# Recurrent heads: the decay levels within 32 tokens computed in 32-column strips of TensorE, in a compact tile

## The chip, the cores and the metric

One core of a Trainium2 chip. The metric is the time of one execution on the device, in microseconds (us); the median of several runs is compared.

## The reference, cut to what matters

The kernel is a decoder trunk on 256 tokens with a model width of 2048: one layer of two parallel head groups, one recurrent layer, and norms around them. The change touches one of the head groups, a gated linear recurrence (16 heads, 128 keys and 128 values each):

```python
def hgrn2(q, fz, v, lb, gain):
    f = lb + (1.0 - lb) * sigmoid(fz)      # decay per key and token
    k = (1.0 - lb) * sigmoid(-fz)
    b = cumsum(log(max(f, TINY)))          # along the tokens of a chunk
    # within a chunk, for s <= t:
    att[t, s] = sum_k silu(q)[t, k] * k[s, k] * exp(b[t, k] - b[s, k])
    o[t] = sum_s att[t, s] * v[s] + what earlier chunks left
```

The decay between two tokens differs for each key, so `att` is no plain product of q and k.

## The kernel before

All weights arrive in chunks of 512 KB, are split by ScalarE (cast, L136) and VectorE (remainder, L137) into two fp32r halves, and are multiplied on TensorE (L183, L185, L209) in units of 256 columns. The order of TensorE's instructions is the order in which the program writes them; the other engines are scheduled by a planner. Side work runs as generators: each `yield n` hands control back, and after n more chunks of the running unit (`tick`, one chunk being about 16 products) the generator goes on. So the small products of a head stand in TensorE's queue between chunks of big ones.

The 16 heads go in 8 pairs, one generator `hgrn` per pair (L670 to L828), with 128 keys on the partitions and four tiles `j` of 128 tokens (two heads, two halves of the 256 tokens). `att` (keys' tokens s on the partitions, four tiles of 128 query tokens t) is built by levels, so that no logarithm is needed. On each level the queries and keys, `qg` and `kg`, carry the decay up to the edge of blocks of w tokens; a product of both gives the entries between neighbouring blocks, and the entries of that level are picked out of the product by a mask. In order: single tokens (L697: diagonal and odd tokens), w=2 and w=8 (L746, three distances at once, in the 192 columns of `qx`), w=32 (L780), w=64 (L791), the far tile (L798). Each of L697 and L746 multiplies all 128 tokens s by 192 columns for each j, in two banks of two tiles, though only entries within blocks of 32 tokens are kept. VectorE picks: L700 and L702 for the single tokens, L769 (six predicated copies a level, whole rows of `att` under masks of 192 columns), L784 for w=32. The level w=64 is copied by ScalarE (L793). Between the products VectorE multiplies `qg` and `kg` by the decays of the level (L738 to L760, `grow` L710 and L711).

fp32 products are recorded as two weight loads and two matmuls each.

Of the kernel before, what the change touches and what calls it, by code (L numbers as in the profile page):

```python
# [9 lines left out]
F32 = mybir.dt.float32  # L10
F32R = mybir.dt.float32r
U8 = mybir.dt.uint8
AF = mybir.ActivationFunctionType
ALU = mybir.AluOpType
# [3 lines left out]
P = 128  # L18
# [17 lines left out]
V_PEK, V_PEV = 240, 272  # L36
NV = 304

C_ID, C_D0, C_D1, C_ROW, C_HEAD, NCONST = 0, 128, 400, 928, 929, 931


def shape_constants():

    c = np.zeros((P, NCONST), np.float32)
    i = np.arange(P)
    c[:, C_ID:C_ID + P] = np.eye(P)

    def follows(w, d):

        n = 4 if d else 2  # L50
        t = i[(i // w) % n >= max(d, 1)]
        return ((i[:, None] // (n * w) == t[None, :] // (n * w)) & (i[:, None] // w == t[None, :] // w - max(d, 1)))

    m = np.zeros((P, 4, 192), np.float32)
    m[:, 0, :64] = follows(1, 0)
    for r, w in ((1, 2), (2, 8)):
        m[:, r] = np.concatenate([follows(w, d) for d in (1, 2, 3)], axis=1)
    m[:, 3, :64] = follows(32, 0)
    ends = np.arange(16) * 16 + 31

    def dist(t, s):
        d = (t[:, None] - s[None, :]).astype(np.float32)
        return np.where(d >= 0, -d, np.float32(NEG))

    cmp0, cmp1 = dist(i, ends), dist(i + P, ends)
    cmp0[:, 15] = cmp1[:, 15] = NEG
    cmp0[:31] = 0.0
    near, far = dist(i, i), dist(i + P, i)
    c[:, C_D0:C_D0 + 272] = np.concatenate([cmp0, near, near], 1)
    c[:, C_D1:C_D1 + 528] = np.concatenate([cmp1, far, far, near, near], 1)  # L70
    c[:, C_ROW] = i >= 31
    for h in range(2):
        c[:, C_HEAD + h] = i // 16 % 2 == h
    return c, m
# [3 lines left out]
def trunk_kernel(ctx: ExitStack, tc: tile.TileContext, x, vecs, consts, blocks, w_in, w_vg, w_out,  # L78
                 w1, w2, o_in, o_gate, o_out, out):
    nc = tc.nc  # L80
    V, S, TE = nc.vector, nc.scalar, nc.tensor

    ctx.enter_context(tc.manual_schedule(engines={mybir.EngineType.PE}))
    cst = ctx.enter_context(tc.tile_pool(name="cst", bufs=1))
# [5 lines left out]
    def bank():  # L90
        return sd.tile([P, 512], F32, name="sb")
# [4 lines left out]
    con = cst.tile([P, NCONST], F32, name="con")  # L96
# [8 lines left out]
    ident = con[:, C_ID:C_ID + P]  # L105
# [263 lines left out]
    cm = tc.alloc_tile_pool(name="cm", bufs=2)  # L369
# [7 lines left out]
            normed(kc[:, 32 * u:32 * u + 32].rearrange("p (g m) b -> p g (m b)", g=2), ps, cm)  # L377
        kcs.append(kc)
    nc.sync.dma_start(con, consts)
    masks = cst.tile([P, 4, 192], U8, name="masks")  # L380
    cst.tile([P, 8], F32, name="pad")

    lb = cst.tile([P, KT], F32, name="lb")
    lb1 = cst.tile([P, KT], F32, name="lb1")
    mk = cm.tile([P, 4, 192], F32, name="mk", bufs=1)
    nc.sync.dma_start(mk, blocks)
    V.tensor_copy(masks, mk)
    e = cm.tile([P, KT], F32, name="e", bufs=1)
# [74 lines left out]
    for br, u0 in ((0, 44), (1, 48)):  # L463
        for u in range(2):
            ps = even_unit(u0 + u)
# [174 lines left out]
    def hgrn_pair(p, ps_f, ps_q):  # L640
# [9 lines left out]
        for h in range(2):  # L650
# [6 lines left out]
        normed(g, ps, hg)  # L657
        s = hg.tile([P, 2, T], F32, name="sg")
        S.activation(s, g, AF.Sigmoid)
        q = hg.tile([P, 4, 192], F32, name="q")  # L660
        V.tensor_tensor(q[:, :, 0:P], g.rearrange("p h (j t) -> p (h j) t", t=P),
                        s.rearrange("p h (j t) -> p (h j) t", t=P), op=ALU.mult)

        v = hg.tile([P, 2, 2 * UC], F32, name="v") if p % 2 == 0 else values[0]
        values[:] = [v]
# [4 lines left out]
    def hgrn(p, q, f, k, v):  # L670
# [1 line left out]
            return t.rearrange("p j (n a w) -> p (j n) a w", a=2, w=w)  # L672


        qe = q[:, :, 0:P].rearrange("p j (n a) -> p j n a", a=2)
        fe = f.rearrange("p j (n a) -> p j n a", a=2)
        qo = q[:, :, P:192]
        qg = hg.tile([P, 4, P], F32, name="qg")
        kg = hg.tile([P, 4, P], F32, name="kg")
        qge = qg.rearrange("p j (n a) -> p j n a", a=2)  # L680
        kge = kg.rearrange("p j (n a) -> p j n a", a=2)
        ke = k.rearrange("p j (n a) -> p j n a", a=2)
        V.tensor_tensor(qo, qe[:, :, :, 1], fe[:, :, :, 1], op=ALU.mult)
        V.tensor_tensor(qge[:, :, :, 0], qe[:, :, :, 0], fe[:, :, :, 0], op=ALU.mult)
        V.tensor_tensor(qge[:, :, :, 1], qo, fe[:, :, :, 0], op=ALU.mult)
        V.tensor_tensor(kge[:, :, :, 0], ke[:, :, :, 0], fe[:, :, :, 1], op=ALU.mult)
        V.tensor_copy(kge[:, :, :, 1], ke[:, :, :, 1])
        gend = hg.tile([P, 4 * 64], F32, name="g2")
        V.tensor_tensor(gend.rearrange("p (j n) -> p j n", j=4), fe[:, :, :, 0], fe[:, :, :, 1], op=ALU.mult)
        att = hg.tile([P, 4, P], F32, name="att")  # L690
        yield 3
        odd = att.rearrange("p j (n a) -> p j n a", a=2)[:, :, :, 1]
        for b in range(2):
            ps = bank()
            for i in range(2):
                j = 2 * b + i
                TE.matmul(ps[:, 192 * i:192 * i + 192], k[:, j], q[:, j], start=(i == 0), stop=(i == 1),  # L697
                          skip_group_check=True)
            pv = ps[:, :384].rearrange("p (j c) -> p j c", j=2)
            V.tensor_tensor(att[:, 2 * b:2 * b + 2], pv[:, :, 0:P],  # L700
                            ident.unsqueeze(1).broadcast_to([P, 2, P]), op=ALU.mult)
            V.copy_predicated(odd[:, 2 * b:2 * b + 2], masks[:, 0, 0:64].unsqueeze(1).broadcast_to([P, 2, 64]),  # L702
                              pv[:, :, P:192])

        def grow(w, gend):

# [9 lines left out]

        for m, w in ((1, 2), (2, 8)):

            n = P // (4 * w)
            qx = hg.tile([P, 4, 192], F32, name="qx")  # L720
            x1_ = qx[:, :, 0:96].rearrange("p j (n c) -> p j n c", n=n)
            x2_ = qx[:, :, 96:160].rearrange("p j (n c) -> p j n c", n=n)
            x3_ = qx[:, :, 160:192].rearrange("p j (n c) -> p j n c", n=n)
            qv = qg.rearrange("p j (n c) -> p j n c", n=n)
            kv_ = kg.rearrange("p j (n c) -> p j n c", n=n)
            gv = gend.rearrange("p (j n a) -> p j n a", j=4, a=4)

            def q_(b):
                return qv[:, :, :, b * w:b * w + w]
# [2 lines left out]
                return kv_[:, :, :, b * w:b * w + w]  # L732

            def g_(b):
                return gv[:, :, :, b:b + 1].broadcast_to([P, 4, n, w])

            S.copy(x1_, qv[:, :, :, w:])
            V.tensor_tensor(x2_[:, :, :, 0:w], q_(2), g_(1), op=ALU.mult)  # L738
            V.tensor_tensor(x2_[:, :, :, w:], q_(3), g_(2), op=ALU.mult)
            V.tensor_tensor(x3_, x2_[:, :, :, w:], g_(1), op=ALU.mult)  # L740
            yield 1
            pss = []
            for h in range(2):
                ps = bank()
                for i in range(2):
                    TE.matmul(ps[:P - w, 192 * i:192 * i + 192], kg[:, 2 * h + i, 0:P - w], qx[:, 2 * h + i],  # L746
                              start=(i == 0), stop=(i == 1), skip_group_check=True)
                pss.append(ps)
            V.tensor_tensor(q_(1), q_(1), g_(0), op=ALU.mult)
            V.tensor_tensor(q_(2), x2_[:, :, :, 0:w], g_(0), op=ALU.mult)  # L750
            V.tensor_tensor(q_(3), x3_, g_(0), op=ALU.mult)
            g2 = hg.tile([P, 3, 4 * n], F32, name=f"g{w}")
            gf = gend.rearrange("p (n a) -> p n a", a=4)
            V.tensor_tensor(g2[:, 0], gf[:, :, 2], gf[:, :, 3], op=ALU.mult)
            V.tensor_tensor(g2[:, 1], gf[:, :, 1], g2[:, 0], op=ALU.mult)
            V.tensor_tensor(g2[:, 2], gf[:, :, 0], g2[:, 1], op=ALU.mult)
            V.tensor_tensor(k_(2), k_(2), g_(3), op=ALU.mult)
            for b in range(2):
                gb = g2[:, 1 - b].rearrange("p (j n) -> p j n", j=4).unsqueeze(3).broadcast_to([P, 4, n, w])
                V.tensor_tensor(k_(b), k_(b), gb, op=ALU.mult)  # L760
            gend = g2[:, 2]
            s1 = P - w
            for h in range(2):
                av = att[:s1, 2 * h:2 * h + 2].rearrange("p j (n c) -> p j n c", n=n)
                pv = pss[h][:s1, 0:384].rearrange("p (j c) -> p j c", j=2)
                c0 = 0
                for d in range(1, 4):
                    cols = 32 * (4 - d)
                    V.copy_predicated(av[:, :, :, d * w:],  # L769
                                      masks[:s1, m, c0:c0 + cols].rearrange("p (n c) -> p n c", n=n).unsqueeze(1)  # L770
                                      .broadcast_to([s1, 2, n, cols // n]),
                                      pv[:, :, c0:c0 + cols].rearrange("p j (n c) -> p j n c", n=n))
                    c0 += cols
            if w == 2:
                yield 1
        yield 1
        ps = bank()
        w = 32
        for j in range(4):
            TE.matmul(ps[:P - w, 64 * j:64 * j + 64], kg[:, j, 0:P - w],  # L780
                      qg[:, j].rearrange("p (n a w) -> p n a w", a=2, w=w)[:, :, 1],
                      start=(j == 0), stop=(j == 3), skip_group_check=True)
        gend = grow(w, gend)
        V.copy_predicated(att[:P - w].rearrange("p j (n a w) -> p j n a w", a=2, w=w)[:, :, :, 1],  # L784
                          masks[:P - w, 3, 0:64].rearrange("p (n w) -> p n w", w=w).unsqueeze(1)
                          .broadcast_to([P - w, 4, 2, w]),
                          ps[:P - w, 0:256].rearrange("p (j n w) -> p j n w", j=4, w=w))
        yield 1
        ps = bank()
        for j in range(4):  # L790
            TE.matmul(ps[:64, 64 * j:64 * j + 64], kg[:, j, 0:64], qg[:, j, 64:128],  # L791
                      start=(j == 0), stop=(j == 3), skip_group_check=True)
        S.copy(att[:64, :, 64:128], ps[:64, :256].rearrange("p (j c) -> p j c", j=4))  # L793
        grow(64, gend)
        yield 1
        ps = bank()
# [232 lines left out]
```

## Time and profile before

| what | value |
|---|---|
| median of 3 runs | 1375.11 us (1373.91 to 1375.12) |
| profiled execution, whole | 1374.71 us |
| its span, first to last instruction | 1372.93 us |
| mean granted TensorE clock over the span | 0.995 |
| stretch of the recurrent heads | 420 to 850 us |

The profiled execution is a run of its own; its span leaves out what lies before the first and behind the last instruction. PE is TensorE's matmuls, PEld its weight loads, DVE VectorE, ACT ScalarE, SP the engine that issues the transfers.

### The profile page before, as it was taken

To read this page: it belongs to the slowest core of one execution; us is meant where nothing else is said; L and a number is where in the kernel's file an instruction comes from. 1 tells how busy PE (TensorE), PEld (TensorE's weight loads), DVE (VectorE), ACT (ScalarE), POOL (GpSimd) and SP (SyncE) were. 2 spreads that over 40 slices of the span, in tenths; PEclk is the share of its full clock that TensorE was granted. 3 is DMA by queue.
4 is the path that set the end of the run, shared out by engine and by line. 5 is a ranking of instruction groups with operands and counts; after the bars stand their busy time and mean duration, and the time that the engine had idled before them with its cause. 6 is when DMAs were issued, how large, how long until landed. Compare 5 with 4: busy or idle time off the path is not lost.

```text
span 1372.9 us, 20842 instructions
## 1 busy us (share of the span) xinstructions
PE 1350.2 (98%) x7970; PEld 1189.9 (87%) x7970; DVE 1030.2 (75%) x1755; ACT 801.4 (58%) x1187; POOL 0.2 (0%) x4
## 2 busy tenths in 40 slices
PE   7999999999999999999999999999999999999996
PEld 6899888988998888888888888888888888888884
DVE  7645478888878765577969687776688988886655
ACT  6435466667664543445444455554559899986442
POOL 0000000000000000000000000000000000000000
PEclk9999999999999999999999999999999999999998
DMA  7765654444445556655445454566665665565662
GB/s 270 249 203 156 195 172 152 154 139 153 140 139 171 187 174 211 191 167 172 140 154 158 149 166 157 187 189 193 197 202 169 188 199 166 184 198 171 185 188 87
DMA packets 77251, 240.93 MB, mean 175 GB/s; under 512 B 7520, under 2 KB 13920, under 8 KB 77152
## 3 DMA queue, kind: packets, MB, share of 16 engines
q1 hardware_dynamic: 77152, 239.61, 55.4%
q8 instruction: 62, 1.02, 0.3%
q14 instruction: 37, 0.30, 0.1%
HBM read 237.48 MB, written 2.10 MB: 174 GB/s over the span
## 4 chain that ended last, share of the span: by engine, by line
PE 96%; DVE 2%; DMA 0%; ACT 0%; issue 0%; SPq 0%; DVEq 0%; ACTq 0%
PE ps L183 50%; PE ps L185 25%; PE ps L209 9%; PE sb L151 2%; PE sb L149 2%; PE sb L150 2%; PE sb L746 2%; PE sb L429 1%; PE sb L552 1%; PE sb L697 1%; DMA wr<-in_w_in 0%; DVE w L137 0%; PE sb L780 0%; DVE part L322 0%; PE sb L791 0%
## 5 line engine op out<-in xcount | busy, mean ns | idle before, releaser
L183 PE MATMUL ps<-hx,w 128*128 128x512 f32 x2176 | 756.5, 400 | 8.6 <-DVE hx L237 7.7
L136 ACT CAST w<-wr 128x1024 fp32r<-128x1024 f32 (+2 forms) x437 | 454.9, 1043 | 499.3 <-PE ps L185 287.1
L137 DVE TENSOR_TENSOR w<-wr,w 128x1024 fp32r<-128x1024 f32 (+2 forms) x437 | 530.7, 1217 | 263.8 <-ACT w L136 262.3
L185 PE MATMUL ps<-hx,w 128*128 128x256 f32 x2176 | 568.6, 280 | 0.5 <-DVE w L137 0.4
L183 PEld LDWEIGHTS ps<-hx,w 128*128 128x128 f32 x2176 | 391.6, 188 | 83.0 <-DVE hx L237 8.2
L185 PEld LDWEIGHTS ps<-hx,w 128*128 128x128 f32 x2176 | 411.4, 189 | 24.1 <-DVE w L137 1.4
L183 PE MATMUL ps<-yx,w 128*128 128x512 f32 x832 | 263.0, 395 | 0.0
L185 PE MATMUL ps<-yx,w 128*128 128x256 f32 x832 | 180.8, 280 | 0.0
L185 PEld LDWEIGHTS ps<-yx,w 128*128 128x128 f32 x832 | 147.0, 188 | 16.0
L183 PEld LDWEIGHTS ps<-yx,w 128*128 128x128 f32 x832 | 142.5, 188 | 20.1
L209 PE MATMUL ps<-w,hx 128*128 128x512 f32 (+1 forms) x576 | 128.0, 377 | 0.0
L209 PEld LDWEIGHTS ps<-w,hx 128*128 128x128 f32 x576 | 100.3, 189 | 17.4
L226 ACT COPY sg<-ps 128x512 f32<-128x512 f32 x68 | 39.3, 578 | 2.0 <-DVE ssum L324 1.2
L528 ACT ACTIVATE pr<-pr,mx 128x16 f32<-128x16 f32 (+2 forms) x96 | 37.8, 396 | 3.3 <-DVE mx L525 3.3
L228 DVE TENSOR_TENSOR tmp<-tmp,rB 128x512 f32<-128x512 f32 x46 | 31.8, 690 | 1.2
L227 DVE TENSOR_TENSOR tmp<-ps,sg 128x512 f32<-128x512 f32 x46 | 31.4, 683 | 0.8 <-ACT sg L226 0.7
L769 DVE COPY_PREDICATED att<-masks,sb 126x192 f32<-126x192 uint8 (+3 forms) x96 | 25.6, 319 | 8.2 <-PE sb L746 7.8
L875 DVE SCALAR_TENSOR_TENSOR xc<-xp,vec,xc 128x256 f32<-128x256 f32 x60 | 25.5, 479 | 0.1
L746 PE MATMUL sb<-qx,kg 128*120 128x192 f32 (+1 forms) x128 | 23.4, 326 | 0.0
L151 PE MATMUL sb<-xch,w 128*128 128x256 f32 x80 | 22.6, 282 | 0.0
L517 DVE SCALAR_TENSOR_TENSOR pr<-con,sb 128x272 f32<-128x272 f32 (+1 forms) x48 | 18.9, 428 | 4.9 <-PE sb L151 4.9
L149 PE MATMUL sb<-xch,w 128*128 128x256 f32 x80 | 22.6, 282 | 0.0
(236 smaller groups left out, 1214.7 us busy)
## 6 DMA issues: line engine op xcount, KB each, us to landing
wr<-in_w_in SPq DMA_DIRECT2D x235, 512.0 KB, 3.8
wr<-in_o_in SPq DMA_DIRECT2D x80, 512.0 KB, 4.2
wr<-in_w_out SPq DMA_DIRECT2D x64, 512.0 KB, 3.7
wr<-in_o_out SPq DMA_DIRECT2D x40, 512.0 KB, 3.6
wr<-in_o_gate SPq DMA_DIRECT2D x10, 512.0 KB, 3.6
w<-in_w SPq DMA_DIRECT2D x8, 512.0 KB, 4.8
wr<-in_w_vg SPq DMA_DIRECT2D x5, 456.0 KB, 3.3
tmp<-in_x SPq DMA_DIRECT2D x8, 256.0 KB, 3.5
```

Source lines behind the costliest of these rows:

```text
L136: S.copy(dst_h, src)
L137: V.tensor_tensor(dst_l, src, dst_h, op=ALU.subtract)
L149: TE.matmul(o, ah, bh, start=start, stop=False, skip_group_check=True)
L151: TE.matmul(o, al, bh, start=False, stop=stop, skip_group_check=True)
L183: TE.matmul(ps[:, n], wk, a, start=(c == 0 and k == 0), stop=stop, skip_group_check=True)
L185: TE.matmul(ps[:, n, 0], wk, a[:, 0], start=False, stop=stop, skip_group_check=True)
L209: TE.matmul(o, a[:, sa, ts], w[:, sw, :, k], start=(c == 0 and k == 0 and i == 0), stop=(c * kc + k == KT - 1 and i == 2), skip_group_chec ...
L226: S.copy(t, ps[:, :, 1])
L227: V.tensor_tensor(dst, ps[:, :, 0], t, op=ALU.add)
L228: V.tensor_tensor(dst, dst, rB2(), op=ALU.mult)
L528: S.activation(branch(h, br), branch(h, br), AF.Exp, bias=mx[:, h, br:br + 1], scale=SCALE, accum_out=zs[:, h, br:br + 1])
L746: TE.matmul(ps[:P - w, 192 * i:192 * i + 192], kg[:, 2 * h + i, 0:P - w], qx[:, 2 * h + i], start=(i == 0), stop=(i == 1), skip_group_chec ...
```

## The change

The entries within blocks of 32 tokens are now computed by blocks alone. q (16 blocks of 32 tokens over the four tiles) and `qx` are laid out as 16 blocks of 48 columns: for each block its 32 tokens and 16 odd ones, or the 48 columns of the three distances. A new function `in_blocks` makes, for each tile j and each block m, a product of the 32 keys' tokens of the block (32 weight columns) with those 48 columns, and puts it on the partitions 32m to 32m+31 of one bank: 16 products of 32 by 48 take the place of four of 128 by 192. The result is compact, 4 tiles of 32 columns, in the new tile `near`; the masks shrink to 48 columns, and each predicated copy serves all four tiles at once. Behind w=8 one VectorE product with a mask of blocks spreads `near` over the whole rows of `att`.

The level w=32 becomes eight products of 32 by 32, on the partitions 0 to 31 and 64 to 95, and two ScalarE copies in the place of the predicated copy L784. The level w=64 keeps its four products, two on the partitions 0 to 63 and two on 64 to 127 in turn, with two ScalarE copies in the place of one. The waits of the generators stay.

```diff
@@ shape_constants
     def follows(w, d):
 
-        n = 4 if d else 2
-        t = i[(i // w) % n >= max(d, 1)]
-        return ((i[:, None] // (n * w) == t[None, :] // (n * w)) & (i[:, None] // w == t[None, :] // w - max(d, 1)))
-
-    m = np.zeros((P, 4, 192), np.float32)
...
+        n, u = 4 if d else 2, i[:32]
+        t = u[(u // w) % n >= max(d, 1)]
+        s = (i % 32)[:, None]
+        return (s // (n * w) == t[None, :] // (n * w)) & (s // w == t[None, :] // w - max(d, 1))
+
+    m = np.zeros((P, 3, 48), np.float32)
...
+    c[:, C_I32:C_I32 + 32] = i[:, None] % 32 == i[None, :32]
+    c[:, C_BLK:C_BLK + 4] = i[:, None] // 32 == i[None, :4]
...
@@ hgrn_pair
-        q = hg.tile([P, 4, 192], F32, name="q")
-        V.tensor_tensor(q[:, :, 0:P], g.rearrange("p h (j t) -> p (h j) t", t=P),
-                        s.rearrange("p h (j t) -> p (h j) t", t=P), op=ALU.mult)
+
+        q = hg.tile([P, 16, 48], F32, name="q")
+        V.tensor_tensor(q[:, :, 0:32], g.rearrange("p h (b t) -> p (h b) t", t=32),
+                        s.rearrange("p h (b t) -> p (h b) t", t=32), op=ALU.mult)
...
@@ hgrn
         att = hg.tile([P, 4, P], F32, name="att")
+        near = hg.tile([P, 4, 32], F32, name="near")
+
+        def in_blocks(kk, qq):
+
+            ps = bank()
+            for j in range(4):
+                for m in range(4):
+                    bs = slice(32 * m, 32 * m + 32)
+                    TE.matmul(ps[bs, 48 * j:48 * j + 48], kk[:, j, bs], qq[:, 4 * j + m], start=(j == 0), stop=(j == 3),
+                              skip_group_check=True)
+            return ps[:, 0:192].rearrange("p (j c) -> p j c", j=4)
+
         yield 3
-        odd = att.rearrange("p j (n a) -> p j n a", a=2)[:, :, :, 1]
-        for b in range(2):
...
+        pv = in_blocks(k, q)
+        V.tensor_tensor(near, pv[:, :, 0:32], con[:, C_I32:C_I32 + 32].unsqueeze(1).broadcast_to([P, 4, 32]),
+                        op=ALU.mult)
+        V.copy_predicated(near.rearrange("p j (n a) -> p j n a", a=2)[:, :, :, 1],
+                          masks[:, 0, 0:16].unsqueeze(1).broadcast_to([P, 4, 16]), pv[:, :, 32:48])
...
-            n = P // (4 * w)
-            qx = hg.tile([P, 4, 192], F32, name="qx")
...
+            n = 32 // (4 * w)
+            qx = hg.tile([P, 16, 48], F32, name="qx")
...
             yield 1
-            pss = []
-            for h in range(2):
-                ps = bank()
...
+            pv = in_blocks(kg, qx)
             V.tensor_tensor(q_(1), q_(1), g_(0), op=ALU.mult)
...
-            for h in range(2):
-                av = att[:s1, 2 * h:2 * h + 2].rearrange("p j (n c) -> p j n c", n=n)
...
+            nv = near.rearrange("p j (n c) -> p j n c", n=n)
+            c0 = 0
+            for d in range(1, 4):
+                cols = 8 * (4 - d)
+                V.copy_predicated(nv[:, :, :, d * w:],
+                                  masks[:, m, c0:c0 + cols].rearrange("p (n c) -> p n c", n=n).unsqueeze(1)
+                                  .broadcast_to([P, 4, n, cols // n]),
+                                  pv[:, :, c0:c0 + cols].rearrange("p j (n c) -> p j n c", n=n))
+                c0 += cols
             if w == 2:
                 yield 1
+
+        V.tensor_tensor(att.rearrange("p j (m t) -> p j m t", m=4), near.unsqueeze(2).broadcast_to([P, 4, 4, 32]),
+                        con[:, C_BLK:C_BLK + 4].unsqueeze(1).unsqueeze(3).broadcast_to([P, 4, 4, 32]), op=ALU.mult)
         yield 1
         ps = bank()
         w = 32
         for j in range(4):
-            TE.matmul(ps[:P - w, 64 * j:64 * j + 64], kg[:, j, 0:P - w],
-                      qg[:, j].rearrange("p (n a w) -> p n a w", a=2, w=w)[:, :, 1],
-                      start=(j == 0), stop=(j == 3), skip_group_check=True)
+            for s0 in (0, 64):
+                TE.matmul(ps[s0:s0 + w, w * j:w * j + w], kg[:, j, s0:s0 + w], qg[:, j, s0 + w:s0 + 2 * w],
+                          start=(j == 0), stop=(j == 3), skip_group_check=True)
+        for s0 in (0, 64):
+            S.copy(att[s0:s0 + w, :, s0 + w:s0 + 2 * w], ps[s0:s0 + w, 0:P].rearrange("p (j t) -> p j t", j=4))
         gend = grow(w, gend)
-        V.copy_predicated(att[:P - w].rearrange("p j (n a w) -> p j n a w", a=2, w=w)[:, :, :, 1],
...
         yield 1
         ps = bank()
-        for j in range(4):
-            TE.matmul(ps[:64, 64 * j:64 * j + 64], kg[:, j, 0:64], qg[:, j, 64:128],
-                      start=(j == 0), stop=(j == 3), skip_group_check=True)
-        S.copy(att[:64, :, 64:128], ps[:64, :256].rearrange("p (j c) -> p j c", j=4))
+        for h in range(2):
+            for j in range(2):
+                TE.matmul(ps[64 * j:64 * j + 64, 64 * h:64 * h + 64], kg[:, 2 * h + j, 0:64], qg[:, 2 * h + j, 64:128],
+                          start=(h == 0), stop=(h == 1), skip_group_check=True)
+        ah = att.rearrange("p (h j) t -> p h j t", j=2)
+        for j in range(2):
+            S.copy(ah[:64, :, j, 64:128], ps[64 * j:64 * j + 64, 0:P].rearrange("p (h c) -> p h c", h=2))
         grow(64, gend)
```

## Rows read from the trace of the kernel before

**Rows 1.** The page, busy time by engine, share of the span, instructions.
```profile
PE 1350.2 (98%) x7970; PEld 1189.9 (87%) x7970; DVE 1030.2 (75%) x1755; ACT 801.4 (58%) x1187; POOL 0.2 (0%) x4
```

**Rows 2.** Waits of TensorE: total us, times, longest.
```profile
PE ps L183 <- DVE hx L237: 7.7, 2, 7.1
PE sb L924 <- ACT sg L948: 1.6, 2, 1.4
```

**Rows 3.** Busy us by engine, 420 to 850 us; behind them clock and DMA.
```profile
420.00:850.00 430.00, 430.00 (x2484) 376.66 (x2483) 324.34 (x665) 205.49 (x259) 0.00 (x0) 1.00 0.54 168
```

**Rows 4.** Chain of waits, first pair of heads: start us, us, what.
```profile
423.86 1.30 PE sb L697 x8
...
427.90 1.30 PE sb L746 x8
...
435.96 2.73 PE ps L209 x12
438.69 0.65 PE sb L780 x8
439.34 2.82 PE ps L209 x12
442.16 0.61 PE sb L791 x8
442.77 0.43 PE ps L183
443.20 0.12 PE ps L185
443.32 0.23 PE ps L183
```

**Rows 5.** TensorE's groups by shape, 400 to 850 us: busy us, mean ns | idle.
```profile
L697 PE MATMUL sb<-q,k 128*128 128x192 f32 x64 | 11.7, 325 | 0.0
L746 PE MATMUL sb<-qx,kg 128*126 128x192 f32 x64 | 11.7, 325 | 0.0
...
L780 PE MATMUL sb<-qg,kg 128*96 128x64 f32 x64 | 6.5, 244 | 0.0
```

**Rows 6.** L791: its durations (ns least/median/most); timeline, from 442.09 and from 442.32.
```profile
L791 PE MATMUL sb<-qg,kg x64: 222/222/270, 442.1 to 829.8; 128*64 128x64 f32 x64
...
442.09 0.68 PE L791 MATMUL sb<-qg,kg 128*64 128x64 f32 x8
442.09 0.54 PEld L791 LDWEIGHTS sb<-qg,kg 128*64 128x64 f32 x8 [0.35 <-issue]
442.32 0.46 PE L791 MATMUL sb<-qg,kg 128*64 128x64 f32 x5
```

**Rows 7.** Chain of waits, products with 128 weight and 66 moving columns.
```profile
58.23 1.83 PE sb L429 x16
```

**Rows 8.** Timeline, 35.2 to 35.75 us: the first products after a wait.
```profile
35.35 0.19 PEld L183 LDWEIGHTS ps<-hx,w 128*128 128x128 f32 x1 [1.02 <-PE sb L311]
35.38 0.47 PE L183 MATMUL ps<-hx,w 128*128 128x512 f32 x1 [0.96 <-DVE kc L227]
```

**Rows 9.** Line 746: weight loads, and the waits its sequencer took up (PEldq).
```profile
L746 PEld LDWEIGHTS sb<-qx,kg x128: 180/186/188, 427.5 to 822.6; 128*126 128x126 f32 x64, 128*120 128x120 f32 x64
...
L746 PEldq EVENT_SEMAPHORE  x20: 51/51/51, 424.6 to 818.5; - x20
```

**Rows 10.** Timeline around L780, first and last pair.
```profile
437.11 0.49 DVE L760 TENSOR_TENSOR kg<-kg,g 128x128 f32<-128x128 f32 x2
...
438.31 0.90 PEld L780 LDWEIGHTS sb<-qg,kg 128*96 128x96 f32 x8
...
824.87 0.49 DVE L760 TENSOR_TENSOR kg<-kg,g 128x128 f32<-128x128 f32 x2
...
825.60 0.79 PEld L780 LDWEIGHTS sb<-qg,kg 128*96 128x96 f32 x8
```

**Rows 11.** VectorE's groups, 420 to 850 us by shape; the first from the page.
```profile
L769 DVE COPY_PREDICATED att<-masks,sb 126x192 f32<-126x192 uint8 (+3 forms) x96 | 25.6, 319 | 8.2 <-PE sb L746 7.8
...
L702 DVE COPY_PREDICATED att<-masks,sb 128x128 f32<-128x128 uint8 x16 | 7.1, 442 | 0.0
L700 DVE TENSOR_TENSOR att<-sb,con 128x256 f32<-128x256 f32 x16 | 7.0, 437 | 0.0
...
L661 DVE TENSOR_TENSOR q<-tmp,sg 128x512 f32<-128x512 f32 x8 | 5.5, 685 | 0.0
...
L769 DVE COPY_PREDICATED att<-masks,sb 126x128 f32<-126x128 uint8 x16 | 4.7, 292 | 0.0
...
L769 DVE COPY_PREDICATED att<-masks,sb 120x64 f32<-120x64 uint8 x16 | 3.6, 226 | 0.2
L784 DVE COPY_PREDICATED att<-masks,sb 96x256 f32<-96x256 uint8 x8 | 3.5, 437 | 0.0
```

More of the change, by code (lines that the diff above doesn't have):

```diff
@@ L37 @@
 NV = 304
-C_ID, C_D0, C_D1, C_ROW, C_HEAD, NCONST = 0, 128, 400, 928, 929, 931
+C_ID, C_D0, C_D1, C_ROW, C_HEAD, C_I32, C_BLK, NCONST = 0, 128, 400, 928, 929, 931, 963, 967
 def shape_constants():
@@ L48, in follows @@
     def follows(w, d):
-        n = 4 if d else 2
-        t = i[(i // w) % n >= max(d, 1)]
-        return ((i[:, None] // (n * w) == t[None, :] // (n * w)) & (i[:, None] // w == t[None, :] // w - max(d, 1)))
-    m = np.zeros((P, 4, 192), np.float32)
-    m[:, 0, :64] = follows(1, 0)
+        n, u = 4 if d else 2, i[:32]
[3 more added lines that the diff above has]
+    m = np.zeros((P, 3, 48), np.float32)
+    m[:, 0, :16] = follows(1, 0)
     for r, w in ((1, 2), (2, 8)):
         m[:, r] = np.concatenate([follows(w, d) for d in (1, 2, 3)], axis=1)
-    m[:, 3, :64] = follows(32, 0)
+    c[:, C_I32:C_I32 + 32] = i[:, None] % 32 == i[None, :32]
+    c[:, C_BLK:C_BLK + 4] = i[:, None] // 32 == i[None, :4]
     ends = np.arange(16) * 16 + 31
@@ L379, in trunk_kernel @@
     nc.sync.dma_start(con, consts)
-    masks = cst.tile([P, 4, 192], U8, name="masks")
-    cst.tile([P, 8], F32, name="pad")
+    masks = cst.tile([P, 3, 48], U8, name="masks")
+    cst.tile([P, 32], F32, name="pad")
     lb = cst.tile([P, KT], F32, name="lb")
     lb1 = cst.tile([P, KT], F32, name="lb1")
-    mk = cm.tile([P, 4, 192], F32, name="mk", bufs=1)
+    mk = cm.tile([P, 3, 48], F32, name="mk", bufs=1)
     nc.sync.dma_start(mk, blocks)
@@ L672, in halves @@
             return t.rearrange("p j (n a w) -> p (j n) a w", a=2, w=w)
-        qe = q[:, :, 0:P].rearrange("p j (n a) -> p j n a", a=2)
-        fe = f.rearrange("p j (n a) -> p j n a", a=2)
-        qo = q[:, :, P:192]
+        qe = q[:, :, 0:32].rearrange("p m (n a) -> p m n a", a=2)
+        fe = f.rearrange("p j (m n a) -> p (j m) n a", n=16, a=2)
+        qo = q[:, :, 32:48]
         qg = hg.tile([P, 4, P], F32, name="qg")
         kg = hg.tile([P, 4, P], F32, name="kg")
-        qge = qg.rearrange("p j (n a) -> p j n a", a=2)
+        qge = qg.rearrange("p j (m n a) -> p (j m) n a", n=16, a=2)
         kge = kg.rearrange("p j (n a) -> p j n a", a=2)
         ke = k.rearrange("p j (n a) -> p j n a", a=2)
+        fk = f.rearrange("p j (n a) -> p j n a", a=2)
         V.tensor_tensor(qo, qe[:, :, :, 1], fe[:, :, :, 1], op=ALU.mult)
@@ L685, in hgrn @@
         V.tensor_tensor(qge[:, :, :, 1], qo, fe[:, :, :, 0], op=ALU.mult)
-        V.tensor_tensor(kge[:, :, :, 0], ke[:, :, :, 0], fe[:, :, :, 1], op=ALU.mult)
+        V.tensor_tensor(kge[:, :, :, 0], ke[:, :, :, 0], fk[:, :, :, 1], op=ALU.mult)
         V.tensor_copy(kge[:, :, :, 1], ke[:, :, :, 1])
         gend = hg.tile([P, 4 * 64], F32, name="g2")
-        V.tensor_tensor(gend.rearrange("p (j n) -> p j n", j=4), fe[:, :, :, 0], fe[:, :, :, 1], op=ALU.mult)
+        V.tensor_tensor(gend.rearrange("p (j n) -> p j n", j=4), fk[:, :, :, 0], fk[:, :, :, 1], op=ALU.mult)
         att = hg.tile([P, 4, P], F32, name="att")
-        yield 3
-        odd = att.rearrange("p j (n a) -> p j n a", a=2)[:, :, :, 1]
-        for b in range(2):
-            ps = bank()
[L695 to L703, printed above, removed]
+        near = hg.tile([P, 4, 32], F32, name="near")
[7 more added lines that the diff above has]
+            return ps[:, 0:192].rearrange("p (j c) -> p j c", j=4)
+        yield 3
+        pv = in_blocks(k, q)
[3 more added lines that the diff above has]
+                          masks[:, 0, 0:16].unsqueeze(1).broadcast_to([P, 4, 16]), pv[:, :, 32:48])
         def grow(w, gend):
@@ L717, in hgrn @@
         for m, w in ((1, 2), (2, 8)):
-            n = P // (4 * w)
-            qx = hg.tile([P, 4, 192], F32, name="qx")
[L721 to L726, printed above, removed]
+            n = 32 // (4 * w)
+            qx = hg.tile([P, 16, 48], F32, name="qx")
+            x1_ = qx[:, :, 0:24].rearrange("p m (n c) -> p m n c", n=n)
+            x2_ = qx[:, :, 24:40].rearrange("p m (n c) -> p m n c", n=n)
+            x3_ = qx[:, :, 40:48].rearrange("p m (n c) -> p m n c", n=n)
+            qv = qg.rearrange("p j (m n c) -> p (j m) n c", m=4, n=n)
+            kv_ = kg.rearrange("p j (m n c) -> p (j m) n c", m=4, n=n)
+            gv = gend.rearrange("p (m n a) -> p m n a", m=16, a=4)
             def q_(b):
@@ L734, in g_ @@
             def g_(b):
-                return gv[:, :, :, b:b + 1].broadcast_to([P, 4, n, w])
+                return gv[:, :, :, b:b + 1].broadcast_to([P, 16, n, w])
             S.copy(x1_, qv[:, :, :, w:])
@@ L741, in hgrn @@
             yield 1
-            pss = []
-            for h in range(2):
[L744 to L748, printed above, removed]
+            pv = in_blocks(kg, qx)
             V.tensor_tensor(q_(1), q_(1), g_(0), op=ALU.mult)
@@ L751, in hgrn @@
             V.tensor_tensor(q_(3), x3_, g_(0), op=ALU.mult)
-            g2 = hg.tile([P, 3, 4 * n], F32, name=f"g{w}")
+            g2 = hg.tile([P, 3, 16 * n], F32, name=f"g{w}")
             gf = gend.rearrange("p (n a) -> p n a", a=4)
@@ L758, in hgrn @@
             for b in range(2):
-                gb = g2[:, 1 - b].rearrange("p (j n) -> p j n", j=4).unsqueeze(3).broadcast_to([P, 4, n, w])
+                gb = g2[:, 1 - b].rearrange("p (m n) -> p m n", m=16).unsqueeze(3).broadcast_to([P, 16, n, w])
                 V.tensor_tensor(k_(b), k_(b), gb, op=ALU.mult)
             gend = g2[:, 2]
-            s1 = P - w
-            for h in range(2):
-                av = att[:s1, 2 * h:2 * h + 2].rearrange("p j (n c) -> p j n c", n=n)
[L765 to L773, printed above, removed]
+            nv = near.rearrange("p j (n c) -> p j n c", n=n)
[7 more added lines that the diff above has]
+                c0 += cols
             if w == 2:
                 yield 1
+        V.tensor_tensor(att.rearrange("p j (m t) -> p j m t", m=4), near.unsqueeze(2).broadcast_to([P, 4, 4, 32]),
+                        con[:, C_BLK:C_BLK + 4].unsqueeze(1).unsqueeze(3).broadcast_to([P, 4, 4, 32]), op=ALU.mult)
         yield 1
```

3 lines of the change are left out of this document (removed).

## Prediction

> **What bounds the kernel now.** I read the page first: TensorE's matmuls are busy for 98% of the span, its weight loads for 87%, VectorE for 75% [rows 1]. A busy matmul engine can still be waiting, so the waits come next: the longest of TensorE's, 7.7 us, falls on a line of the first norm, long before the change, and the next, 1.6, on the last norm, long after it [rows 2]. [...] Last the chain of waits through one pair of heads, which gives the price of every block of products that the change touches, in place [rows 4].
>
> **What the old products cost.** Each fp32 product is two weight loads and two matmuls in the records, so a level's four products per pair of heads stand as x8; 64 records over eight pairs are one block each [rows 5]. The token-diagonal level and the levels w=2 and w=8 take 1.30 us each [rows 4]: 162 ns a record for 192 moving columns, 0.85 ns a column, so there the moving side sets the pace. The w=32 level takes 0.65 us, and the products behind it 0.08 more than the same twelve take elsewhere (2.82 against 2.74): 0.73 us [rows 4]. With the other pairs, some of which lose less behind it, I take 0.71. The w=64 level takes 0.61, and the product behind it 0.43 in place of 0.23: 0.81 us [rows 4].
>
> The w=64 block shows more. It is the one whose output has 64 partitions. Its steady pace is (0.46 - 0.222)/4, about 58 ns a record [rows 6], so 8 records explain 0.47 of 0.81; the weight loads stood idle for 0.35 us before it, with nothing awaited [rows 6], while the other blocks' loads run under the matmul before. I read 0.34 us per block as the price of going over to half an array and back. [...]
>
> **What the new products cost.** Per pair of heads each of the three levels becomes 16 products of 32 weight columns and 48 moving columns, 32 records; w=32 becomes 8 products of 32 by 32, 16 records; w=64 keeps 8 records but puts neighbours in different halves of the array. So three blocks and the w=32 block now pay for a change of mode too. In 32 columns its first exposed weight load is shorter by about 25 ns, so I take 0.31 us for each.
>
> Pace of one record, from rows. Weights: 128 columns take 1.83/16 = 114 ns [rows 7] and 64 take 58 [rows 6], so 32 take about 30. Moving: 48 x 0.85 = 41, with a few ns of gap 45. What no row shows is whether a product in one strip runs beside one in another, for every product before sits in the same columns as its neighbour. This is the open cost:
>
> - No overlap: 45 ns a record, the slower of the two sides. The level costs 32 x 45 + 310 = 1.75 us against 1.30.
> - Full overlap: the two records of one product share a strip and follow each other (45 ns in all), then the next strip may start. 16 x 45 + 310 = 1.03 us.
> - Overlap, but fed by the sequencer. After an empty queue a matmul started 30 ns behind its weight load [rows 8], whereas with a filled queue both start together [rows 6]; so one instruction takes the sequencer about 30 ns. A wait of the first w=2 block was taken up at 424.6 for loads at 427.5 [rows 9], twelve pairs ahead at 229 ns; the last at 818.5, for a block that begins at about 821.5, seventeen pairs at 172 ns. So the queue holds about 33 instructions. A level now has 64: 33 are there, 31 x 31 ns = 0.96 us must pass for the rest. 0.96 + 0.31 = 1.27 us, 0.03 less than before.
> - A floor: the shortest pace on record is 58 ns [rows 6]. If that is a price per record and not that of 64 columns, a level costs 32 x 58 + 310 = 2.17 us.
>
> I take the third. Weight loads and matmuls already run beside each other in one half array (58 ns, not their sum), so the array does take separate work at once, and the 30 ns row is the only one of an unfilled queue. The choice between overlap and none has no row at all, which is why both ends stay in the range.
>
> With the third: three levels -0.03 each, -0.09. Level w=32: the sequencer is held by VectorE's last factor until about 0.7 us before the block [rows 10], so some 22 of 32 instructions are ready when its products start; 10 x 31 + 310 = 0.62 against 0.71, -0.09. Level w=64: its 16 instructions are all in the queue, and two halves overlap: 0.23 in place of 0.47, -0.23. Sum -0.41 us per pair, -3.3 us for eight.
>
> **The other engines.** VectorE loses the diagonal product (437 ns twice), the first predicated copy (about as long, twice), 12 copies (25.6 us over all pairs) and the w=32 copy (437 ns) [rows 11], some 43 us. It gains a product and seven shorter copies of 32 to 128 elements, at 0.22 to 0.3 us as rows of 64 to 128 elements show [rows 11], and a spread over 512 elements of SBUF at about 0.69 [rows 11], 2.7 us a pair. That is 21 us less on an engine with 106 idle us in the stretch [rows 3]: I cost it at nothing, since TensorE waits for it nowhere there. ScalarE gains three short copies a pair beside 225 idle us [rows 3], also nothing. Two of them wait for the spread and for the w=32 block, and weight casts stand behind them in ScalarE's queue; a cast that is late by less than a tick is hidden by the weight buffers ahead of TensorE, which wait on nothing in the stretch; without that cover it would cost its wait, a few tenths of a us a pair. One margin is thin: VectorE's last factor before w=32 ends at 437.60 and is wanted at 438.31, in the last pair at 825.36 and 825.60 [rows 10]. These factors keep their counts of elements, and follow the end of the w=8 block as before, so the margin stays; if their new layout cost 20 ns more each, nine of them would take 0.18 of the 0.24 us. The other new thing queued behind them, the spread, is wanted only by the last products of the head, several ticks later. The smaller masks and the slightly longer constants are loaded before 40 us, where nothing waits for them: nothing either way.
>
> **The rivals.**
> 1. *Strips take turns.* 1.75 against 1.30 three times, +1.35; w=32 16 x 30 + 310 = 0.79 against 0.71, +0.08; w=64 unchanged. +1.43 us a pair, +11.4 us: 1386.5. For it: the moving side is one stream wherever a row shows it, 0.85 ns a column. Against: nothing that a row shows. It decides from 31 ns a record up (that is where 32 records and the change of mode reach 1.30).
> 2. *Full overlap, the queue keeps up.* 1.03, -0.27 three times; w=32 8 x 32 + 310 = 0.57, -0.14; w=64 -0.23. -1.18 a pair, -9.4: 1365.7. For it: load and matmul start together when the queue is full [rows 6]. Against: the 30 ns of rows 8. [...]
> 3. *A floor for every small product.* 2.17 against 1.30, +0.87 three times; w=32 16 x 58 + 310 = 1.24, +0.53; +3.13 a pair, +25.0: 1400.1. For it: 58 is the shortest pace on record; against: 64 columns alone explain it. [...]
> 4. *Matmuls overlap, weight loads go in single file.* 30 ns a record: levels 1.27, w=32 0.79, w=64 unchanged: -0.1 us, 1375.0. The change then does nothing for the time.
>
> **How the numbers follow.** The sum is made against the profiled execution: 1374.71 us, of which 1372.93 are the span and 1.8 lie around it. -3.3 gives 1371.4; the median of the runs is 0.40 above that execution, so 1371.8. Chances: the forecast 0.32, full overlap 0.22, loads in file 0.08, turns 0.25, a floor 0.13. A measurement of this kernel tells a change from none at about 0.2%, 2.75 us. The forecast lies just beyond that, so I split it 0.19 faster to 0.13 same. Faster: 0.22 + 0.19 = 0.41. Same: 0.13 and 0.06 of loads in file: 0.19. Slower: 0.25 + 0.13 + 0.02 = 0.40. The range leaves out the floor and little else: from 1.5 under full overlap to some 2 over turns, 1364 to 1389. The forecast's own range is 1369 to 1374.
>
> **What would show it.** In the chain, a level's block as x32 at about 0.96 us plus a first product behind it of 0.43 in place of 0.23; starts 30 ns apart in its second half if the sequencer feeds it, evenly 45 if strips take turns, 58 if there is a floor; pairs of starts 41 ns and a few ns apart if strips overlap in full. Idle time of the weight loads before each of the five narrow blocks of a pair (0.3 us) shows the change of mode, and its absence would make me wrong by up to 0.3 x 32 = 10 us to the good. VectorE busy about 20 us less, with TensorE still without idle time between 420 and 850 us; a wait for a factor at w=32 would show the thin margin gone. [...]

## Result and profile after

The changed kernel takes 1358.32 us (median of 4 runs, 1358.12 to 1359.10) against 1375.11 in the same comparison: a ratio of 0.9879, 95% interval 0.9868 to 0.9891, or 16.8 us less. The forecast was 1371.8, its range 1364 to 1389. The sign was right, the size lies below the range.

The page of the changed kernel, busy time by engine [rows 1]:
```profile
span 1356.3 us, 22071 instructions
## 1 busy us (share of the span) xinstructions
PE 1333.5 (98%) x8610; PEld 1165.7 (86%) x8610; DVE 1011.4 (75%) x1691; ACT 807.2 (60%) x1211; POOL 0.2 (0%) x4
```
TensorE has 640 records more, 80 for each pair of heads, and is busy for 16.7 us less; the span is 16.6 us shorter. Its waits and the stretch of the heads, the first view as in [rows 2], the second as in [rows 3]:
```profile
PE ps L185 <- DVE hx L239: 7.8, 2, 7.5
PE sb L928 <- ACT sg L952: 1.6, 2, 1.4
...
415.00:850.00 435.00, 435.00 (x3237) 368.56 (x3236) 322.77 (x626) 223.03 (x297) 0.00 (x0) 1.00 0.55 176
```
The waits are the old ones. TensorE never stands still while the heads run (busy for 435.00 us of 435.00), at the same granted clock of 1.00. So the time went where TensorE's own blocks became shorter. The chain of waits through the first pair, to be laid beside [rows 4]:
```profile
424.57 0.48 PE sb L703 x32
425.04 2.99 PE ps L211 x12
428.04 0.48 PE sb L703 x32
428.51 5.77 PE ps L211 x24
434.28 0.48 PE sb L703 x32
434.76 2.99 PE ps L211 x12
437.75 0.38 PE sb L784 x16
438.12 3.00 PE ps L211 x12
441.12 0.38 PE sb L793 x8
441.50 0.43 PE ps L185
```
L703 is the line of `in_blocks`, L784 the level w=32, L793 w=64. A level within 32 tokens shows 0.48 us where it showed 1.30, and the twelve products behind it 2.99 in place of 2.73; w=32 and w=64 show 0.38 in place of 0.65 and 0.61. From the start of the last big product ahead to that of the second behind, less the usual distances of big products, all 24 blocks of the three levels cost 0.67 to 0.69 us, w=32 0.57 to 0.58, w=64 about 0.58. Before it was 1.30, 0.71 and 0.81. Summed over the eight pairs: 24 x 0.62 + 8 x 0.14 + 8 x 0.23 = 17.8 us.

That is 1.2 more than the span lost. Both kernels hold the same 6592 big products, so each can be followed from the old trace to the new one: 0.3 us are lost ahead of the first and 0.3 more up to 420 us, the stretch of the heads (420 to 845 us) becomes shorter by 15.8 and not by 17.8, and behind it another 1.4 are gained. The differences lie in the distances of the big products, which moved by a few ns in every stretch, with and without heads: neighbouring L211 products of 512 columns stand 232 ns apart where L209 stood 228, while the L185 and L187 pairs behind 850 us became about 1 ns shorter on average. These distances came back in every kernel built from the changed one. Why they moved was not tried.

The durations of the new records, and the first block in the timeline:
```profile
L703 PEld LDWEIGHTS sb<-q,k x256: 106/110/110, 424.5 to 797.9; 128*32 128x32 f32 x128
L703 PE MATMUL sb<-q,k x256: 206/206/231, 424.5 to 798.0; 128*32 128x48 f32 x128
...
424.49 0.41 PEld L703 LDWEIGHTS sb<-q,k 128*32 128x32 f32 x32 [0.36 <-issue]
424.50 0.55 PE L703 MATMUL sb<-q,k 128*32 128x48 f32 x32
...
424.97 0.50 PE L211 MATMUL ps<-w,hx 128*128 128x512 f32 x1
```
All 32 matmuls start within 0.55 - 0.206 = 0.34 us, 11 ns apart on average, where the profile has one take 206 ns from end to end: in these records many are on their way at once. Asked up to 424.55 us and up to 424.60, the timeline holds four of them and then eight:
```profile
424.50 0.25 PE L703 MATMUL sb<-q,k 128*32 128x48 f32 x4
424.50 0.29 PE L703 MATMUL sb<-q,k 128*32 128x48 f32 x8
```
The single records show four starts 7 ns apart, the next four 67 ns after the first four, and from then on four more every 42.5 ns. A record does not name its strip; with products written to the four strips in turn, two records each, I read one start per strip in every group of four. The weight loads stood idle for 0.36 us before the block with nothing awaited, as [rows 6] showed 0.35 for w=64. I read this as the price of going over to a part of the columns and back, which I call the change of mode; no run shows what it consists of. Less the 0.34 of starts, a block's 0.67 to 0.69 us leave about 0.33 for it.

VectorE's side, by shape, to be laid beside [rows 11]:
```profile
L777 DVE TENSOR_TENSOR att<-near,con 128x512 f32<-128x512 f32 x8 | 5.5, 688 | 0.2
L769 DVE COPY_PREDICATED near<-masks,sb 128x96 f32<-128x96 uint8 x16 | 4.4, 276 | 0.0
L769 DVE COPY_PREDICATED near<-masks,sb 128x64 f32<-128x64 uint8 x16 | 3.6, 224 | 0.3
L769 DVE COPY_PREDICATED near<-masks,sb 128x32 f32<-128x32 uint8 x16 | 3.3, 208 | 0.4
L711 DVE COPY_PREDICATED near<-masks,sb 128x64 f32<-128x64 uint8 x8 | 2.4, 298 | 0.0
L709 DVE TENSOR_TENSOR near<-sb,con 128x128 f32<-128x128 f32 x8 | 2.3, 285 | 0.0
```
2.7 us a pair as worked out. Over the span VectorE is busy for 1011.4 us in place of 1030.2, 18.8 less where 21 were worked out.

### The profile page after: what moved, and what is told of

The parts are those of the page before. It is cut to its first block, busy times and chain, and to the rows that moved or that the text cites. A ratio compares the mean times of both kernels' runs of the same rounds, so it can differ in the third digit from the quotient of the medians.

```text
span 1356.3 us, 22071 instructions
## 1 busy us (share of the span) xinstructions
PE 1333.5 (98%) x8610; PEld 1165.7 (86%) x8610; DVE 1011.4 (75%) x1691; ACT 807.2 (60%) x1211; POOL 0.2 (0%) x4
## 4 chain that ended last, share of the span: by engine, by line
PE 97%; DVE 2%; DMA 0%; ACT 0%; issue 0%; SPq 0%; DVEq 0%; ACTq 0%
PE ps L185 51%; PE ps L187 26%; PE ps L211 9%; PE sb L153 2%; PE sb L151 2%; PE sb L152 2%; PE sb L431 1%; PE sb L703 1%; PE sb L554 1%; DVE w L139 0%; DMA wr<-in_w_in 0%; PE ps L153 0%; PE ps L152 0%; PE ps L151 0%; DVE x L963 0%; DVE part L324 0%
## 5 line engine op out<-in xcount | busy, mean ns | idle before, releaser
L185 PE MATMUL ps<-hx,w 128*128 128x512 f32 x2176 | 754.0, 397 | 8.8 <-DVE hx L239 7.8
L187 PE MATMUL ps<-hx,w 128*128 128x256 f32 x2176 | 572.9, 282 | 0.0
L185 PEld LDWEIGHTS ps<-hx,w 128*128 128x128 f32 x2176 | 391.9, 188 | 80.1 <-DVE hx L239 8.3
L187 PEld LDWEIGHTS ps<-hx,w 128*128 128x128 f32 x2176 | 410.1, 188 | 23.1 <-DVE w L139 0.5
L185 PE MATMUL ps<-yx,w 128*128 128x512 f32 x832 | 263.9, 396 | 0.0
L187 PE MATMUL ps<-yx,w 128*128 128x256 f32 x832 | 180.3, 279 | 0.0
L187 PEld LDWEIGHTS ps<-yx,w 128*128 128x128 f32 x832 | 147.1, 188 | 16.7
L185 PEld LDWEIGHTS ps<-yx,w 128*128 128x128 f32 x832 | 142.1, 188 | 20.7
L211 PE MATMUL ps<-w,hx 128*128 128x512 f32 (+1 forms) x576 | 129.8, 380 | 0.0
L211 PEld LDWEIGHTS ps<-w,hx 128*128 128x128 f32 x576 | 99.6, 188 | 20.1
L152 PE MATMUL sb<-xcl,w 128*128 128x256 f32 x80 | 22.6, 283 | 0.0
```

Of the source, the lines that this page charges most:

```text
L152: TE.matmul(o, ah, bl, start=False, stop=False, skip_group_check=True)
L185: TE.matmul(ps[:, n], wk, a, start=(c == 0 and k == 0), stop=stop, skip_group_check=True)
L187: TE.matmul(ps[:, n, 0], wk, a[:, 0], start=False, stop=stop, skip_group_check=True)
L211: TE.matmul(o, a[:, sa, ts], w[:, sw, :, k], start=(c == 0 and k == 0 and i == 0), stop=(c * kc + k == KT - 1 and i == 2), skip_group_chec ...
```

## Experiments

Theory A, formed from these rows: the four strips work at once, each takes its own records one after the other at 42.5 ns (48 columns at 0.85 ns and a little), and a block costs the longest strip plus 0.33 us for going over to strips and back. Its rivals stand in the expectations.

**One strip, and two.**
```diff
-                    TE.matmul(ps[bs, 48 * j:48 * j + 48], kk[:, j, bs], qq[:, 4 * j + m], start=(j == 0), stop=(j == 3),
+                    os = slice(32 * (m % 1), 32 * (m % 1) + 32)      # second kernel: m % 2
+                    TE.matmul(ps[os, 48 * j:48 * j + 48], kk[:, j, bs], qq[:, 4 * j + m], ...
```


> All 16 products of a level go to the first column strip (partitions 0 to 31 of the bank, the four blocks of a tile added up there); the count, the shapes and the other engines' work stay, but the blocks' entries are lost, so the recurrent heads' output changes. Theory A, strips work beside each other and each strip takes its own records one after the other: 32 records at 42.5 ns = 1.36 us plus 0.33 for the change of mode, 1.01 us more than the changed kernel in each of 24 blocks, +24 us: about 1382.5 us. Rival B, a record of a narrow product takes about 11 ns wherever it lands: 1358 us.

> The 16 products of a level go to two strips in turn, blocks 0 and 2 added up in the first, 1 and 3 in the second (the output of the heads changes). Theory A: 16 records a strip at 42.5 ns = 0.68 us plus 0.33, 0.34 us more in each of 24 blocks, +8.2 us: about 1366.5 us. Rival B: 1358 us.

Measured: 1382.67 us with one strip, 1366.14 with two (four: 1358.3). The first block in the timeline, one strip and then two:
```profile
424.73 1.55 PE L704 MATMUL sb<-q,k 128*32 128x48 f32 x32
```
```profile
424.62 0.87 PE L704 MATMUL sb<-q,k 128*32 128x48 f32 x32
```
Less the 0.206 of the last one, the starts span 1.34, 0.66 and 0.34 us for one, two and four strips. Of TensorE's work only the strip of the output differs, and that the blocks are added up there; VectorE's picking copies shrink to that strip's partitions. The adding up is not what costs: with one strip a record starts every 42.5 ns, and so do the records of one strip in the order by strips below, where the products of a strip go to different columns. With one strip the kernel is slower than the old one (ratio 1.0057, 1.004 to 1.0074): this is the prediction's first rival, near its price. Rival B falls.

**Twice the products.**
```diff
+            for r in (192, 0):
             for j in range(4):
                 for m in range(4):
-                    TE.matmul(ps[bs, 48 * j:48 * j + 48], ...
+                    TE.matmul(ps[bs, r + 48 * j:r + 48 * j + 48], ...
```


> Every level's 16 products are made twice, the first time into columns of the bank that nothing reads: 64 records, 128 instructions a block. Theory A, the strips set the pace: 8 records more a strip, +0.34 us in each of 24 blocks, +8.2 us: about 1366.5 us. Rival C, the sequencer needs 30 ns an instruction and a block of 64 instructions only just fits the queue: 64 more at 30 ns, +1.9 us a block, +46 us: about 1404 us, with starts 30 ns apart in the second half of a block.

Measured: 1366.49 us. The first block:
```profile
424.60 0.89 PE L704 MATMUL sb<-q,k 128*32 128x48 f32 x64
```
64 loads and 64 matmuls start in 0.68 us, one instruction every 5 ns, and the second half as fast as the first. A sequencer at 30 ns an instruction, the term that the prediction built on, is excluded, unless the queue held all 128 instructions ahead, where the prediction's own reading gave it about 33.

**The written order.** Three kernels with the same products in other orders.
```diff
-            for j in range(4):
-                for m in range(4):
+            for m in range(4):                                  # strip by strip
+                for j in range(4):
```
```diff
+            for j, m in [(2 * h + i, m) for h in range(2) for m in range(4) for i in range(2)]:            # pairs
+            for j, m in [(j, m) for js in ((0, 1, 2), (3,)) for m in range(4) for j in js]:                # triples
```


> Same products, but written strip by strip: the four tiles of strip 0, then of strip 1 and so on, so that eight records in a row share a strip. Theory A1, the queue lets a strip's records pass those of a strip that is busy: the four strips still overlap, about 1358 us. Rival A2, matmuls start in the order written: each strip's eight records take 0.34 us and only the last overlaps the next strip, 1.3 us a block, +23 us: about 1381 us.

Measured: 1372.62 us, neither. The block spans
```profile
425.02 1.13 PE L703 MATMUL sb<-q,k 128*32 128x48 f32 x32
```
In the written order the four strips would take 8 records each in turn, 4 x 0.33 = 1.3 us of starts; it is 1.13 - 0.206 = 0.92. Asked up to 425.21 us and up to 425.225, the timeline holds four records and then six:
```profile
425.02 0.36 PE L703 MATMUL sb<-q,k 128*32 128x48 f32 x4
425.02 0.43 PE L703 MATMUL sb<-q,k 128*32 128x48 f32 x6
```
One of the two is the first strip's fifth, 0.195 us after its first; the other, 6 ns behind it, cannot share its strip, where a record starts only every 42.5 ns. Read by these distances, each strip begins 0.20 us after the one before, 6 ns after that one's fifth record of eight. So, by this reading, later strips do pass waiting records, but not freely. I took this for a window of four records in all, and the order by pairs was to test it.

> Same products, written two tiles of a strip at a time, so that four records in a row share a strip. The order by strips (eight in a row) cost 0.58 us a block, and its starts fit a queue in which a matmul may start ahead of up to three that wait for their strip. Theory A3, just that: worked through for this order, the last start comes 0.18 us later than in the changed kernel, +4.3 us over 24 blocks: about 1362.6 us. Rival A4, the queue looks as far as it likes and the order by strips lost its time in something else (a later weight load for each strip): 1358 us. Rival A2, half of what the order by strips lost: 1365 us.

Measured: 1359.87 us, so A3 falls: 1.3 more than the changed kernel on the same chip (1358.53), not 4. The first block of the pairs in the timeline:
```profile
425.47 0.58 PE L703 MATMUL sb<-q,k 128*32 128x48 f32 x32
```
In the single records the starts span 0.38 us, 0.04 more than in the changed kernel, where A3 gave 0.18 more; all four strips begin 13 ns apart, the fourth with nine of the records written ahead of it not yet started. An estimate that fits the starts of both orders is a short queue at each strip, which no record shows: three wait behind the one that runs, and the fourth holds up everything written after it. By it little is held up with four records in a row; with eight, the next strip begins when the fifth starts. Triples, six in a row, were to test it.

> Same products, written three tiles of a strip at a time and then the fourth tiles, so that six records in a row share a strip. Theory A5, formed after the order by pairs: records are handed out in the written order, each strip keeps up to three waiting behind the one that runs, and a full strip holds up all that is written behind. Worked through: the strips begin 0.11 us apart and the last start comes 0.32 us later than in the changed kernel, +7.7 us: about 1366.2 us. Rival A4, the order hardly matters beyond the time to hand out the records: 1359 to 1360 us. Rival A2, matmuls start in the order written, a strip's six after the other: 0.7 us more a block, 1375 us.

Measured: 1366.54 us. The first block of the triples in the timeline:
```profile
424.71 0.87 PE L703 MATMUL sb<-q,k 128*32 128x48 f32 x32
```
0.87 - 0.206 = 0.66 us of starts, 0.32 more than the changed kernel, as worked out ahead of the run. Rival A2's 0.7 us more a block does not fit this run either.

**VectorE's load put back.**
```diff
         grow(64, gend)
+        dm = hg.tile([P, 4, P], F32, name="dm", bufs=1)
+        for _ in range(4):
+            V.tensor_tensor(dm, kg, kg, op=ALU.mult)
```


> VectorE gets four more products of 512 elements for each pair of heads, into a tile that nothing reads, some 22 us in all: about what the change took from it. Theory A, TensorE alone sets the time in this stretch: 1358.5 us as the changed kernel. Rival E, VectorE's relief gave part of the gain: up to some us more.

Measured: 1358.56 us, ratio to the kernel before 0.9879, as the change alone. VectorE is busy for 340.88 us of the stretch in place of 322.77:
```profile
415.00:850.00 435.00, 435.00 (x3236) 368.56 (x3235) 340.88 (x658) 224.21 (x298) 0.00 (x0) 1.00 0.55 175
```
Between the same two big products, at 400 us and at 845 us, this trace and that of the changed kernel take equally long to 0.01 us. The added products stand in one place, behind w=64, and not where the old copies stood; as much VectorE work as the change took away costs nothing there.

**The three levels alone.**
```diff
-            for s0 in (0, 64):
-                TE.matmul(ps[s0:s0 + w, w * j:w * j + w], kg[:, j, s0:s0 + w], qg[:, j, s0 + w:s0 + 2 * w], ...
+            TE.matmul(ps[:P - w, 64 * j:64 * j + 64], kg[:, j, 0:P - w], ...
...
+        for j in range(4):
+            TE.matmul(ps[:64, 64 * j:64 * j + 64], kg[:, j, 0:64], qg[:, j, 64:128], ...
```


> Only the three levels within 32 tokens are changed: w=32 is made by four products of 96 weight columns again and w=64 by four in the first half of the array (ScalarE copies both). Theory A: w=32 costs 0.71 again in place of 0.57, w=64 0.81 in place of 0.58, +0.36 us for each of 8 pairs, +2.9 us: about 1361.4 us. If those two parts gave nothing: 1358.5 us.

Measured: 1363.13 us, 4.6 more where 2.9 were expected. The blocks cost what was expected: w=32 0.71 (0.79 in the last pair), w=64 0.81, together 3.0 us more. In the last pair the w=32 block waited for VectorE's last factor, the margin that the prediction called thin. The weight loads there, in this kernel and in the changed one:
```profile
813.43 0.76 PEld L783 LDWEIGHTS sb<-qg,kg 128*96 128x96 f32 x8 [0.15 <-DVE kg L763]
```
```profile
810.85 0.33 PEld L784 LDWEIGHTS sb<-qg,kg 128*32 128x32 f32 x16 [0.24 <-DVE kg L763]
```
The factor ends 0.05 us before the loads here and 0.15 in the changed kernel, where [rows 10] has 0.24 before the change. In the changed kernel the block nevertheless costs 0.57 as in the other pairs: its loads would stand idle about as long for the change of mode alone, as those of w=64 did in the last pair before the change (0.25, with nothing awaited).

The rest of the 4.6 has a place of its own, in the waits of TensorE:
```profile
PE ps L187 <- DVE w L139: 1.1, 2, 0.8
```
It is a wait for split weights at 1177 and 1181 us, in the recurrent layer that follows, absent there from both traces of the changed kernel. Two products start 1.24 and 0.69 us behind the one before in place of 0.23, and the product behind each comes 0.1 later than usual, together 1.7. So w=32 and w=64 bring 3.0 us where they stand; the wait I cannot assign to them from one trace.

**One entry less.** The single-token block moved to stand directly ahead of the w=2 block.
```diff
-        pv = in_blocks(k, q)
...
             yield 1
+            if w == 2:
+                p0 = in_blocks(k, q)
             pv = in_blocks(kg, qx)
```


> The single-token block is moved behind the next wait of the generator, directly ahead of the w=2 block: the same products, but one entry into narrow strips and one return less for each pair of heads. Theory A, each entry and return together cost 0.33 us whatever lies between: 8 x 0.33 = 2.6 us less, about 1355.7 us. Rival D, the 0.33 us are the start-up of each block's own products (its first weights, its own wait): 1358.3 us.

> The changed kernel again, for comparison on the same chip: 1358.3 us.

Measured on one chip: merged 1355.61 us (1355.35 to 1355.95), changed 1358.53 (1358.00 to 1359.03), 2.9 less. The merged block in the chain:
```profile
427.45 0.82 PE sb L703 x64
428.26 5.79 PE ps L211 x24
```
0.82 for both levels in place of 0.48 twice, and one slow return (5.79) in place of two. In these runs the price hangs on the entry into strips and the return, not on a block's products: rival D falls.

**Four strips for w=32, on top of it.**
```diff
+                r0, c0 = s0 + w * (j % 2), w * (j // 2)
+                TE.matmul(ps[r0:r0 + w, c0:c0 + w], kg[:, j, s0:s0 + w], qg[:, j, s0 + w:s0 + 2 * w], ...
```


> As the merged one, and the eight w=32 products are spread over four strips in place of two (four copies on ScalarE in place of two). Theory A, the strips set the pace: four records a strip in place of eight, 0.1 us less in each of 8 blocks, 0.8 us beyond the merge: about 1354.9 us. If the two strips of w=32 were not what sets its pace: as the merged one.

Measured: 1355.11 us (1355.07 to 1355.36), ratio to the kernel before 0.9857 (0.9842 to 0.9872). The w=32 block with two strips and with four:
```profile
437.45 0.45 PE L786 MATMUL sb<-qg,kg 128*32 128x32 f32 x16
```
```profile
438.01 0.33 PE L787 MATMUL sb<-qg,kg 128*32 128x32 f32 x16
```
0.12 us shorter a block; over the eight pairs, between the same big products ahead of and behind the heads, the trace is 0.9 shorter than the merged one's. 0.5 of it stands in the medians, whose runs just touch. This is the fastest version that was run.

## Why the prediction was right or wrong

- *What bounds the kernel, VectorE's saving set at nothing*: right. TensorE is busy for all 435.00 us from 415 to 850 us, and with VectorE's load put back the time is 1358.56 us, as without it.
- *The price of a change of mode, 0.31 us, paid by four blocks more a pair*: right. 0.32 to 0.35 in the changed kernel, 0.33 in the levels within 32 tokens; 2.9 us for eight entries less in the merged one, 0.36 each.
- *The pace of a record, 41 to 45 ns from rows of 192 columns*: right, 42.5 in the one-strip kernel. That kernel also plays the first rival, turns: 1386.5 was worked out, 1382.67 measured, with w=32 and w=64 left overlapping.
- *"The two records of one product share a strip and follow each other (45 ns in all), then the next strip may start"*: wrong, and this is the step that failed for the range. The next strip starts 7 ns later, while the second record still waits (it starts 67 ns behind the first); four strips work at once. The term of 16 x 45 ns = 0.72 us measured 0.34, so even "full overlap" was set at 1.03 us a level where 0.68 was measured. The lower end of the range was taken from it, and the time fell outside.
- *"Overlap, but fed by the sequencer"*, the case chosen: wrong, and this is the step that failed for the forecast. Its term of 31 x 31 ns = 0.96 us a level measured 0.34. The 30 ns between one load and its matmul after a wait [rows 8] is no rate: 128 instructions went at 5 ns each, and the matmul of that row is listed with a wait of its own, for L227. The choice cost three levels 0.59 us each: forecast -0.03, measured -0.62, 14.2 us over 24 blocks.
- *w=32 and w=64*: -0.09 forecast and -0.14 measured, -0.23 and -0.23. At w=64 the reason held too: the two halves overlap, 0.23 us of starts for 8 records. At w=32 the sum came close by luck, from the same wrong rate (10 x 31 ns); the two strips took 0.25 us of starts.
- *VectorE and ScalarE at nothing, the thin margin at w=32*: right for the time; no wait of TensorE was added. The margin did not stay as it was: in the last pair it went from 0.24 us to 0.15, and in the kernel with the three levels alone to 0.05, where it cost 0.08. VectorE's part was tried, ScalarE's only seen in the trace.
- *A floor of 58 ns, loads in single file*: neither; loads start as close together as matmuls (in the first block four of each within 20 ns).

## What to carry to other kernels

Small fp32 products like these, whose entries are needed only on a block diagonal, are worth cutting into column strips when TensorE sets the time: four strips worked at once here (0.34 us of starts a block, 1.34 with one strip), and a block cost the longest strip's records plus about a third of a microsecond for going over and back. Write neighbours into different strips, no more than four records of a strip in a row (0.38 us of starts, six took 0.66), and put narrow blocks directly behind one another, so that the change is paid once (2.9 us less for eight changes). A price read off a single pair of instructions, such as one late start after a wait, should enter a sum only as an end of the range.

## What the hardware showed unexpectedly

- In the changed kernel fp32 matmuls in different column strips start 6 to 7 ns apart, each strip going on at 42.5 ns for 48 columns (four strips) and 32 ns for 32 (two strips). Only a strip's second record comes later, 67 and 52 ns behind its first; why was not tried.
- Orders with 2, 4, 6 and 8 records of a strip in a row give starts over 0.34, 0.38, 0.66 and 0.92 us. An estimate from these traces, 3.3 ns to hand out a record (half the step between strips in the changed kernel) and three records waiting at each strip, gives 0.34, 0.36, 0.66 and 0.92, with the 67 and 42.5 ns between a strip's records; with two waiting the order of six would take 0.79, with four 0.53. The 0.32 us that the order of six adds were worked out ahead; that it is such a queue is argued from these times, not seen.
- Going over to strips and back cost 0.32 to 0.36 us, for 32-column and 64-column strips alike, and changing from one strip to another nothing that shows: four strips start within 20 ns.
- The distances of the big products moved by a few ns with the new kernel (4 on average at L211), in both directions, also where nothing was changed; the cause is open.
